# A two-layer diffusion trunk on one core: head products that take turns, attention in turns with dense projections, and one modulation round and the filter spectra at other places

## The chip, the cores and the metric

The kernel runs on one core of one Trainium2 chip. The metric is the time of one execution in device microseconds (us), a median over runs; lower is better. Below, PE is the matrix engine and PEld its weight loads, DVE the vector engine, ACT the scalar engine, POOL the general engine, and SP the engine whose queue issues nearly all DMAs.

## The reference, cut to what matters

Two trunk layers run over 256 latent tokens and 256 context tokens of width 1024. A layer is: modulation, one input projection whose columns go to attention, RWKV-7 and Hyena, one output projection, a norm, a channel mixer (dense SwiGLU in layer 0, top-2-of-8 experts in layer 1), a norm.

```python
for l in range(DEPTH):                      # DEPTH = 2
    need_ctx = l < DEPTH - 1
    mod_l = (cond_lat @ ada_w[l] + ada_b[l])[:, None, :]      # six vectors of 1024: sh1 sc1 g1 sh2 sc2 g2
    mod_c = (cond_ctx @ ada_w[l] + ada_b[l])[None, None, :]
    o_lat, o_ctx = token_mixer(modulate(x, sh1, sc1), modulate(xc, csh1, csc1), lp, rope, need_ctx)
    x = post_norm(alpha * x + g1 * o_lat, ln1_g[l], ln1_b[l])
    ...                                     # context: the same, in layer 0 alone
    f_lat = swiglu(...) if l % 2 == 0 else moe_swiglu(...)
    x = post_norm(alpha * x + g2 * f_lat, ln2_g[l], ln2_b[l])

def token_mixer(h_lat, h_ctx, lp, rope, need_ctx):
    u_lat = h_lat @ lp['w_in']; u_ctx = h_ctx @ lp['w_in']
    att_l, att_c = attention_group(...)     # latent queries read latent and context keys
    rw_l, rw_c = rwkv_group(...)            # latent scans start from the context scans' last states
    hy_l = hyena_group(u_lat[..., s_hy], lp)   # long convolution by spectra of filters (hyena_filter_spectrum)
    o_lat = jnp.concatenate([att_l, rw_l, hy_l], -1) @ lp['w_out']
    ...
```

## The kernel before, in words

Dense products are done in three passes of a split: `split` (L314 to L316) cuts an f32 operand into a high part (a cast on ACT, L315) and a rest (a subtraction on DVE, L316), and `mm3` (L318) sends three matmuls, L321, L322 and L323. `wload` fetches 512 KB of weights into a raw buffer (`raw`, L347, SP's queue) and splits it. The raw buffers are rings: six in the stage "l" (all of layer 0 and layer 1's context), five in the stage "n" (layer 1's latent mixer), thirty in the expert stage. `behind` keeps the order of loads in SP's queue as written. The order of the instructions on an engine is fixed when the kernel is built: a scheduler goes by the order in which the code emits them and by its own estimate of what is ready, so work emitted nearby is mixed. On the chip every engine runs its own list strictly in order.

What the tiles are called:

- `ada(l, rounds)` (L372) makes the modulation vectors: a round is 16 weight loads, each with four plain f32 matmuls of 32 weight columns (L392), a DVE addition, and four transposes `adaT`. `s.fill` hands such a round to `wload`, which takes one step of it with each weight load.
- `win_steps` (L466) is the input projection by tiles of 128 columns (`u`, 24 matmuls per tile). RW, ATT and HY are the tile lists of the three mixers; HY tiles are followed by a short convolution.
- `attend` (L755) yields after each half of a head pair: scores `aS`, the maximum on DVE, an exponential on ACT (`aP`), transposes `aPT`, the product with the values `ao`, the normaliser `azb`. A yield ends a turn where `go` (L1635) alternates several generators.
- `rw_dir` (L882) is one direction of RWKV: the triangular solve, then per token tile the chunk matrices `rM` (L1063) and `rN` (L1071, L1073), the serial scan `rS` (L1089), and `rZ` and `rY` (L1105 to L1124). It is run eight times, and each run does `rN` for two token tiles and four heads: 64 head turns in all. Two heads of a pair write to partitions 0 to 63 and 64 to 127 of one bank.
- `spectra(l, ...)` (L534) makes the filter spectra: `hf_d`, `hf`, two sines (`sn`, seven DVE instructions and one on ACT each), `hf_n`, `Kc`, `Ks`, `Kn`; it needs only weights, no token.
- `w_out` (L1295) is the output projection (`wo`) with its norm; `ffn` is the dense channel mixer (`ab`, then `fo`); `hT` (L445) normalises, transposes (L455) and splits an input.

Two calls of the RWKV code, `rwkv(0, ...)`, stand in layer 0 for the latent tokens and for the context, and two in layer 1. The calls around the change are all in `body` (L1676).

Of the kernel before, what the change touches and what calls it, by code (L numbers as in the profile page):

```python
# [251 lines left out]
CTX, LAT = 0, 1  # L252


def bc(ap, shape):
    return ap.to_broadcast(list(shape))
# [556 lines left out]
class Rwkv(Mix):  # L813
# [73 lines left out]
    def rw_dir(s, l, g, d, need_y):  # L887
# [3 lines left out]
        mm = nc.tensor.matmul  # L891
# [5 lines left out]
        for ct in range(2):  # L897
            for i in range(2):
                mm(ps[:, ct, i], g["th"][:, i, 256 * d + 128 * ct:256 * d + 128 * ct + 128], cum[:, d, :], start=True,
                   stop=True)  # L900
# [5 lines left out]
        for ct in range(2):  # L906
            mm(ps[:, ct], s.lora[l][32:64, 1, 256 * d + 128 * ct:256 * d + 128 * ct + 128], g["lora"][32:64, :],
               start=True, stop=True)
# [25 lines left out]
        for p in range(2):  # L934
            b = s.bank(f"w{d}", "rAB").rearrange("p (u m t) -> p u m t", u=4, m=4)
            r = slice(64 * p, 64 * p + 64)
            for tt in range(2):
                for ct in range(2):
                    for j in range(4):
                        o = slice(128 * tt + 32 * j, 128 * tt + 32 * j + 32)  # L940
                        for m, lh in ((0, kd), (2, be)):
                            mm(b[32 * j:32 * j + 32, 2 * tt + ct, m:m + W, :], lh[r, ct, o], kr[r, 0:W, ct, o],
                               start=True, stop=True)
# [13 lines left out]
        x = sub[:, 768:896].rearrange("p (u t) -> p u t", u=8)  # L957
# [19 lines left out]
        hv = lambda h: slice(64 * h, 64 * h + 64)  # L977
# [3 lines left out]
        kdt, bet = kbt[:, 0], kbt[:, 1]  # L981
        for tt in range(2):
            o = slice(128 * tt, 128 * tt + 128)
            b = s.bank(f"w{d}", "rtr")
# [5 lines left out]
        b = s.bank(f"w{d}", "rtr").rearrange("p (a c) -> p a c", a=2)  # L990
# [6 lines left out]
        b = s.bank(f"w{d}", "rAV").rearrange("p (i h v) -> p i h v", i=2, h=4)  # L997
# [10 lines left out]
        for i in range(1, 16):  # L1008
            t = i if d == 0 else 15 - i
# [14 lines left out]
        PQ = s.k([128, 2, 4, 2, 64], f"rPQ{d}")  # L1024
        done = [last]
        for step, w in enumerate((TT, BC, TT)):
            rhs = PQ if step == 1 else KA
            for tt in range(2):
                b = s.bank(f"w{d}", "rPQ")
                for h in range(4):  # L1030
                    mm(b[:, 128 * h:128 * h + 128], w[:, U(tt, h), :], rhs[:, tt, h].rearrange("p m v -> p (m v)"),
                       start=True, stop=True)
# [9 lines left out]
        bx = [s.k([128, 4, 256], f"rbx{d}") for _ in range(2)]  # L1042
        vx = g.get("vx")
        if vx is None:
            vx = g["vx"] = [s.k([128, 4, 256], "rvx") for _ in range(2)]
# [11 lines left out]
        for tt in range(2):  # L1057
            x = M[tt]
            s.order(nc.gpsimd.memset(x, 0.0), done[MX[tt]])
            b = s.bank(f"w{d}", "rM").rearrange("p (c j k) -> p c j k", c=2, j=4)  # L1060
            for h in range(4):
                r = slice(64 * (h % 2), 64 * (h % 2) + 64)
                mm(b[r, h // 2], PQ[:, tt, h, 0, :], bx[tt][:, :, hv(h)], start=True, stop=True)  # L1063
            for p in range(2):
                r = slice(64 * p, 64 * p + 64)
                nc.vector.tensor_add(x[r, :, r], b[r].rearrange("p c j k -> p (c j) k"),
                                     bc(s.c("ident")[r, r][:, None, :], [64, 8, 64]))
            b = s.bank(f"w{d}", "rN").rearrange("p (c j k) -> p c j k", c=2, j=4)
            for h in range(4):
                r = slice(64 * (h % 2), 64 * (h % 2) + 64)  # L1070
                mm(b[r, h // 2], kdt[:, tt, hv(h)], vx[tt][:, :, hv(h)], start=True, stop=True)  # L1071
                for j in range(4):
                    mm(b[r, h // 2, j, :], bx[tt][:, j, hv(h)], PQ[:, tt, h, 1, :], start=False, stop=True,  # L1073
                       skip_group_check=True)
            fed = nc.vector.tensor_mul(N[:, tt], b, bc(gc[:, :, 4 * tt:4 * tt + 4, None], [128, 2, 4, 64]))

        S = s.k([128, 8, 2, 64], f"rS{d}")
# [1 line left out]
        start = {}  # L1079
        prev = g["S0"][d] if g["S0"] else None  # L1080
        for i, ch in enumerate(order):
            tt, j = divmod(ch, 4)
# [3 lines left out]
            else:  # L1086
                b = s.bank(f"w{d}", "rS")[:, :128].rearrange("p (c v) -> p c v", c=2)
# [13 lines left out]
        b = s.bank(f"w{d}", "rZ").rearrange("p (c t) -> p c t", c=2)  # L1101
        for tt in range(2):
            for h in range(4):
                r = slice(64 * (h % 2), 64 * (h % 2) + 64)
                mm(b[r, h // 2, 128 * tt:128 * tt + 128], PQ[:, tt, h, 0, :], BD[3][:, U(tt, h), :], start=True,  # L1105
                   stop=True)
# [3 lines left out]
        for p in range(2):  # L1110
            b = s.bank(f"w{d}", "rY")[:, :256].rearrange("p (i c v) -> p i c v", i=2, c=2)
            r = slice(64 * p, 64 * p + 64)
            for tt in range(2):
                for ct in range(2):
                    h = 2 * ct + p
                    i = mm(b[:, tt, ct, :], BD[1][:, U(tt, h), :], vt[:, tt, hv(h)], start=True, stop=True)
                    if tt == 0 and ct == 0:
# [3 lines left out]
                       skip_group_check=True)  # L1121
                    for j in chs:
                        c0 = 128 * tt + 32 * j
                        mm(b[32 * j:32 * j + 32, tt, ct, :], Z[r, ct, c0:c0 + 32], start[4 * tt + j][r, ct, :],  # L1124
                           start=False, stop=True, skip_group_check=True)
# [77 lines left out]
class Ffn(Rwkv):  # L1203
# [63 lines left out]
        return ms, rs, last  # L1267

    def tok_mm(s, src, ts, banks, nk, khs=None):

        for n, kh in enumerate(khs or range(nk // 2)):
            hi, lo = s.wload(src(kh))
            if n == s.LAG:
                s.flush()
            for i in range(len(banks))[::1 - 2 * (kh % 2)]:
                for k in (2 * kh, 2 * kh + 1):
                    ns = slice(512 * (k % 2), 512 * (k % 2) + 512)
                    s.mm3(banks[i], ts(i, k), (hi[:, ns], lo[:, ns]), k == 0, k == nk - 1)

    def tok_last(s, chunks, ts, nk):  # L1280

# [10 lines left out]
        if f:  # L1292
            f()

    def w_out(s, l, st, oT, x, halves=False):  # L1295


        ts = lambda i, k: tuple(t[:, 128 * i:128 * i + 128] for t in oT[k])
        banks = []

        def product(h, khs=None):
            s.tok_mm(lambda kh: s.A["wout"][l, h, kh], ts, banks[h], 8, khs)

        def o(h):
            if halves:
                banks.append([s.bank("g", "wo") for _ in range(2)])
                product(h)
            elif h == 0:
                banks.extend([[s.bank("g", "wo") for _ in range(2)], [s.bank(f"w{i}", "wo") for i in range(2)]])
                for h2 in range(2):  # L1310
                    product(h2, [0, 1, 2])
                s.tok_last([(s.A["wout"][l, h2, 3], 3, banks[h2]) for h2 in range(2)], ts, 8)
            yield
            return banks[h]

        return s.whole(s.post_norm(l, st, 0, x, [o], () if halves else (0, 1)))


    def block(s, b, hp):
# [248 lines left out]
class Top(Ffn):  # L1568
# [58 lines left out]
    def whole(s, gen):  # L1627

        while True:
            try:  # L1630
                next(gen)
            except StopIteration as e:
                return e.value

    def go(s, *gens):  # L1635

        gens = [g if isinstance(g, tuple) else (1, g) for g in gens]
        while gens:
            for q in list(gens):
                for _ in range(q[0]):  # L1640
                    if next(q[1], s) is s:
                        gens.remove(q)
                        break
# [14 lines left out]
    def body(s):  # L1658
        RW, HY, ATT = [0, 1, 2, 3, 4, 7, 8], [13, 14, 15, 16, 17, 18], [5, 6, 9, 10, 11, 12]
        s.setup()  # L1660
        s.w = "a"
        ada = s.ada(0, [0])
        s.some(ada, 3)
        s.ldcst(1)
        s.some(ada, 5)
        with s.behind():
            x = s.ldx(CTX)
        for _ in ada:
            pass
        s.w = "l"  # L1670
        sp = s.spectra(0, "w0", "t", "w1", *s.sp)
        next(sp)
        oT = []
        s.ldlora(0)

        def start(st, x):  # L1676
            g = {"st": st, "h": s.hT(0, st, 0, x)}
            if st == 0:
                next(sp)
            oT.append(s.pairs("oTa", "oTa", "oTr", "oTh"))  # L1680
            s.win(0, RW, g)
            for n in (3, 4) if st == 0 else ():
                s.ldcst(n)
            return g


        g = start(CTX, x)
        s.rw_prep(0, g)
        s.win(0, HY, g)
        S0 = s.rwkv(0, g, None, oT[CTX])  # L1690
        s.fill = s.ada(0, [1, 2])
        s.go(s.hyena(0, g, oT[CTX]))
        s.win(0, ATT, g)
        with s.behind():
            x = s.ldx(LAT)

        gl = start(LAT, x)
        s.go(s.attend(0, g, oT[CTX]))
        s.rw_prep(0, gl)
        s.win(0, HY, gl)  # L1700
        s.rwkv(0, gl, S0, oT[LAT])
        s.win(0, ATT, gl)
        s.go(s.attend(0, gl, oT[LAT]))
        x = [s.w_out(0, CTX, oT[CTX], None, True)]
        s.go(s.hyena(0, gl, oT[LAT]))
        s.drain()
        f = s.ffn(0, CTX, x[CTX])
        s.some(f, 1)
        x.append(s.w_out(0, 1, oT[1], None))
        s.fill = s.ada(1, [0, 1, 2])  # L1710
        xc = s.whole(f)
        s.drain()
        f = s.ffn(0, LAT, x[LAT])
        s.some(f, 10)

        s.ldlora(1)
        gc = {"st": CTX, "h": s.hT(1, CTX, 0, xc)}
        s.win(1, [0, 1, 2, 3, 4, 5, 6], gc)
        s.rw_prep(1, gc)
        S0 = s.rwkv(1, gc, None, None)  # L1720
        sp = s.spec_load(1)
        x = s.whole(f)

        s.w = "n"
        gl = {"st": LAT, "h": s.hT(1, LAT, 0, x)}
        for _ in s.spectra(1, "w0", "t", "w1", *sp()):
            pass
        oT = s.pairs("oTa", "oTa", "oTr", "oTh")
        s.win(1, RW, gl)
        s.rw_prep(1, gl)  # L1730
        s.rwkv(1, gl, S0, oT)
        s.win(1, ATT + HY[:2], gl)
        s.go(s.attend(1, gl, oT))
        s.win(1, HY[2:], gl)
        s.go(s.hyena(1, gl, oT))
        x = s.w_out(1, LAT, oT, x)
        s.w = "m"
        s.moe(1, x)
# [18 lines left out]
```

## Time and profile before

| | us |
|---|---|
| median of 3 runs | 2132.26 |
| lowest and highest | 2120.98, 2132.55 |
| the profiled execution: its time, its span | 2140.86, 2139.1 |

Its mean granted clock of PE is 0.959 of full speed. In the rows, a window is a stretch in us from the span's start, and it gives the busy time of each engine in it (number of instructions), the granted clock, the share of the DMA engines and GB/s. PE's matmuls overlap, so the mean duration of one is longer than the step from one to the next.

### The profile page before, as it was taken

Reading aid. Unit: us, or ns where it says so; the run is one execution under the profiler, and the core shown is the slowest. Engines: PE = TensorE matmul, PEld = TensorE weight load, DVE = VectorE, ACT = ScalarE, POOL = GpSimd, SP = SyncE. Lnnn points to the kernel's source line nnn. Section 1 sums busy time; section 2 is a strip of 40 time slices with the busy share of each in tenths; the row PEclk is TensorE's granted clock in tenths of the full one; section 3 lists DMA queues with packets and bytes.
Section 4 is the critical chain, followed back from the end, with each engine's and each line's share of the span. In section 5 each row is a group of like instructions: output and inputs, shape, how many; then the busy total and the mean of one; then the engine's idle time right before and its main releaser. Section 6 shows DMA issues by size and latency. Waiting matters only on the chain. (4 is left out here: it accounts for less than half of the span.)

```text
span 2139.1 us, 35418 instructions
## 1 busy us (share of the span) xinstructions
PE 2044.7 (96%) x13514; PEld 1668.0 (78%) x13514; DVE 1659.1 (78%) x3050; ACT 1102.6 (52%) x1613; POOL 106.2 (5%) x87
## 2 busy tenths in 40 slices
PE   8999999999999999989798997999999999999996
PEld 3878777768877999978577676888888888888885
DVE  7786678459744595685888568799899989998997
ACT  3532445132333434443354232777787877778773
POOL 0022001100000000010002200000000000000000
PEclk9999899799999999999898997999999999999998
DMA  8422333146698535422311038699999999999992
GB/s 323 164 82 90 139 124 82 59 155 223 231 341 298 197 131 198 165 83 95 128 60 53 30 110 315 216 322 361 355 346 367 354 341 351 366 356 342 364 353 105
DMA packets 147850, 469.12 MB, mean 219 GB/s; under 512 B 31636, under 2 KB 33972, under 8 KB 147672
## 3 DMA queue, kind: packets, MB, share of 16 engines
q1 hardware_dynamic: 123512, 446.27, 57.6%
q0 software_dynamic: 4816, 17.36, 2.2%
q10 hardware_dynamic: 19344, 3.15, 0.8%
q8 instruction: 108, 1.77, 0.3%
q14 instruction: 70, 0.57, 0.1%
HBM read 464.56 MB, written 2.16 MB: 218 GB/s over the span
## 5 line engine op out<-in xcount | busy, mean ns | idle before, releaser
L316 DVE TENSOR_TENSOR wlo<-wraw,whi 128x1024 fp32r<-128x1024 f32 x748 | 885.3, 1219 | 87.4 <-ACT whi L315 58.7
L315 ACT CAST whi<-wraw 128x1024 fp32r<-128x1024 f32 x748 | 751.2, 1049 | 132.8 <-DMA wraw<-in_fw_dram 39.0
L321 PE MATMUL ab<-whi,m_x 128*128 128x512 f32 x704 | 281.6, 400 | 0.0
L323 PE MATMUL ab<-whi,m_x 128*128 128x512 f32 x704 | 275.6, 391 | 0.0
L322 PE MATMUL ab<-wlo,m_x 128*128 128x512 f32 x704 | 275.0, 391 | 0.0
L321 PE MATMUL ab<-hp,whi 128*128 128x256 f32 x704 | 205.2, 293 | 3.1 <-ACT hp L315 2.2
L323 PE MATMUL ab<-hp,wlo 128*128 128x256 f32 x704 | 201.7, 288 | 4.0 <-DVE wlo L316 4.0
L322 PE MATMUL ab<-hp,whi 128*128 128x256 f32 x704 | 201.5, 287 | 1.3 <-DVE hp L316 1.1
L321 PE MATMUL u<-hp,whi 128*128 128x256 f32 x512 | 153.7, 303 | 2.7 <-ACT hp L315 2.5
L323 PEld LDWEIGHTS ab<-whi,m_x 128*128 128x128 f32 x704 | 132.2, 188 | 28.3
L322 PEld LDWEIGHTS ab<-wlo,m_x 128*128 128x128 f32 x704 | 132.5, 188 | 25.5 <-DVE wlo L316 0.2
L321 PEld LDWEIGHTS ab<-whi,m_x 128*128 128x128 f32 x704 | 132.2, 188 | 25.1
L323 PE MATMUL u<-hp,wlo 128*128 128x256 f32 x512 | 150.8, 297 | 1.0 <-DVE wlo L316 1.0
L322 PE MATMUL u<-hp,whi 128*128 128x256 f32 x512 | 151.4, 298 | 0.0
L321 PEld LDWEIGHTS ab<-hp,whi 128*128 128x128 f32 x704 | 136.2, 194 | 18.9 <-issue 11.0
L323 PEld LDWEIGHTS ab<-hp,wlo 128*128 128x128 f32 x704 | 136.4, 194 | 5.8 <-DVE wlo L316 5.3
L322 PEld LDWEIGHTS ab<-hp,whi 128*128 128x128 f32 x704 | 136.7, 194 | 2.0 <-DVE hp L316 1.8
L321 PE MATMUL mo<-whi,ffg 128*128 128x512 f32 x352 | 137.8, 392 | 0.0
L323 PE MATMUL mo<-whi,ffg 128*128 128x512 f32 x352 | 137.1, 390 | 0.0
L322 PE MATMUL mo<-wlo,ffg 128*128 128x512 f32 x352 | 137.0, 389 | 0.0
L321 PEld LDWEIGHTS u<-hp,whi 128*128 128x128 f32 x512 | 101.2, 199 | 18.7 <-issue 10.3
L969 POOL TENSOR_TENSOR rBD<-rAT,cst 128x1024 f32<-128x1024 f32 x28 | 66.3, 2373 | 889.7 <-issue 523.5
(396 smaller groups left out, 3550.5 us busy)
## 6 DMA issues: line engine op xcount, KB each, us to landing
wraw<-in_mw_dram SPq DMA_DIRECT2D x495, 512.0 KB, 5.6
wraw<-in_fw_dram SPq DMA_DIRECT2D x132, 512.0 KB, 5.5
wraw<-in_adaw_dram SPq DMA_DIRECT2D x96, 512.0 KB, 4.7
wraw<-in_win_dram SPq DMA_DIRECT2D x64, 512.0 KB, 4.8
wraw<-in_mw_dram POOLq DMA_DIRECT2D x33, 512.0 KB, 6.8
wraw<-in_wout_dram SPq DMA_DIRECT2D x24, 512.0 KB, 4.3
lngb<-in_rows_dram SPq DMA_DIRECT2D x12, 512.0 KB, 7.1
x<-in_xs_dram SPq DMA_DIRECT2D x8, 512.0 KB, 5.4
```

Of the source, the lines that this page charges most:

```text
L315: i = (s.nc.scalar.copy if eng == "a" else s.nc.vector.tensor_copy)(hi, src)
L316: return i, s.nc.vector.tensor_sub(lo, src, hi.bitcast(F32))
L321: mm(out, a[0], b[0], start=start, stop=False, **kw)
L322: mm(out, a[0], b[1], start=False, stop=False, **kw)
L323: mm(out, a[1], b[0], start=False, stop=stop, **kw)
L969: i = nc.gpsimd.tensor_mul(x.rearrange("p u (j t) -> p u j t", j=4), bc(ATu[:, :, m, None, :], [128, 8, 4, 32]), bc(mask.rearrange("p (j t ...
```

## The change

Five things change. First, in `rw_dir` the four heads' `rN` products are written so that the two heads of a pair alternate matmul by matmul. Second, `w_out` can be run in steps (`w_out_steps`, over `tok_steps`; a turn is one weight load), and `into` stores its result. Third, attention takes turns with a dense projection in three places: the context's attention of layer 0 with the latent HY tiles (the attention stood before `rw_prep`), the latent attention of layer 0 with the context's output projection (which followed it), and the latent attention of layer 1 with all six HY tiles (two of them stood before it, four behind). Fourth, the third round of layer 1's `ada` is no longer part of the filling of the context's channel mixer, but runs at once where the latent channel mixer has ended. Fifth, layer 1's spectra, with all their loads, are emitted before the rest of the latent channel mixer, no longer behind the latent `hT` of layer 1.

```diff
             b = s.bank(f"w{d}", "rN").rearrange("p (c j k) -> p c j k", c=2, j=4)
-            for h in range(4):
-                r = slice(64 * (h % 2), 64 * (h % 2) + 64)
-                mm(b[r, h // 2], kdt[:, tt, hv(h)], vx[tt][:, :, hv(h)], start=True, stop=True)
+            for c in range(2):
+                for p in range(2):
+                    h = 2 * c + p
+                    mm(b[64 * p:64 * p + 64, c], kdt[:, tt, hv(h)], vx[tt][:, :, hv(h)], start=True, stop=True)
                 for j in range(4):
-                    mm(b[r, h // 2, j, :], bx[tt][:, j, hv(h)], PQ[:, tt, h, 1, :], start=False, stop=True,
-                       skip_group_check=True)
+                    for p in range(2):
+                        h = 2 * c + p
+                        mm(b[64 * p:64 * p + 64, c, j, :], bx[tt][:, j, hv(h)], PQ[:, tt, h, 1, :], start=False,
+                           stop=True, skip_group_check=True)
...
     def tok_mm(s, src, ts, banks, nk, khs=None):
+        for _ in s.tok_steps(src, ts, banks, nk, khs):
+            pass
+
+    def tok_steps(s, src, ts, banks, nk, khs=None):
         for n, kh in enumerate(khs or range(nk // 2)):
             hi, lo = s.wload(src(kh))
...
                     s.mm3(banks[i], ts(i, k), (hi[:, ns], lo[:, ns]), k == 0, k == nk - 1)
+            yield
...
+    def into(s, out, gen):
+        out.append((yield from gen))
...
         gl = start(LAT, x)
-        s.go(s.attend(0, g, oT[CTX]))
         s.rw_prep(0, gl)
-        s.win(0, HY, gl)
+        s.go(s.attend(0, g, oT[CTX]), s.win_steps(0, HY, gl))
         s.rwkv(0, gl, S0, oT[LAT])
         s.win(0, ATT, gl)
-        s.go(s.attend(0, gl, oT[LAT]))
-        x = [s.w_out(0, CTX, oT[CTX], None, True)]
+        x = []
+        s.go(s.attend(0, gl, oT[LAT]), s.into(x, s.w_out_steps(0, CTX, oT[CTX], None, True)))
...
-        s.fill = s.ada(1, [0, 1, 2])
+        s.fill = s.ada(1, [0, 1])
...
         S0 = s.rwkv(1, gc, None, None)
-        sp = s.spec_load(1)
+        for _ in s.spectra(1, "w0", "t", "w1", *s.spec_load(1)()):
+            pass
         x = s.whole(f)
+        for _ in s.ada(1, [2]):
+            pass
         s.w = "n"
         gl = {"st": LAT, "h": s.hT(1, LAT, 0, x)}
-        for _ in s.spectra(1, "w0", "t", "w1", *sp()):
-            pass
...
-        s.win(1, ATT + HY[:2], gl)
-        s.go(s.attend(1, gl, oT))
-        s.win(1, HY[2:], gl)
+        s.win(1, ATT, gl)
+        s.go(s.attend(1, gl, oT), s.win_steps(1, HY, gl))
```

Three places of the built order. On PE, in the `rN` of the first direction in layer 0's latent RWKV, before (lines of the kernel before, `rM`, `aS`, `ada` and `aPT` being other work that the scheduler put between):

```order
L392 MATMUL ada_2934<-wraw_4606,keep_66 32x256
L1063 MATMUL rM_3462<-rbx0_3409,rPQ0_3371 64x256 x3
L774 MATMUL aS_4324<-akv_1866,aq_4052 128x512
L774 MATMUL aS_4325<-akv_1866,aq_4052 128x512
L1063 MATMUL rM_3462<-rbx0_3409,rPQ0_3371 64x256
L392 MATMUL ada_2934<-wraw_4606,keep_66 32x256 x3
L1071 MATMUL rN_3469<-rvx_3411,rkbt0_3265 64x256
L1073 MATMUL rN_3469<-rPQ0_3371,rbx0_3409 64x64 x4
```

The same `rN` tile in the changed kernel, whose lines are L1073 for the wide product and L1077 for the narrow ones:

```order
L392 MATMUL ada_2812<-wraw_4289,keep_66 32x256 x4
L321 MATMUL wo_4281<-whi_4285,oTa_392 128x512
L1073 MATMUL rN_3469<-rvx_3411,rkbt0_3265 64x256 x2
L1077 MATMUL rN_3469<-rPQ0_3371,rbx0_3409 64x64 x6
L774 MATMUL aS_4307<-akv_1866,aq_4052 128x512
L774 MATMUL aS_4308<-akv_1866,aq_4052 128x512
L1077 MATMUL rN_3469<-rPQ0_3371,rbx0_3409 64x64 x2
```

Before, one head's wide and four narrow products stood together, and the next head's behind them; now two wide ones stand together, and eight narrow ones in which the heads alternate.

On PE, from the last matmul of layer 0's latent channel mixer (`fo`) to the first products of layer 1's latent projection (`u`), before:

```order
L323 MATMUL fo<-whi,ffg 128x512
L542 MATMUL hf_10450<-cst_68,sn 64x256
L548 MATMUL hf_d<-hydec,cst_68 128x512
L563 MATMUL hf_d<-hyd,cst_68 128x512
L557 MATMUL hf_10471<-sn 64x256
L455 MATMUL hT<-keep,xhat 128x128 x2
L575 MATMUL hf_10490<-hy_10446,sn 128x512
L455 MATMUL hT<-keep,xhat 128x128 x6
L575 MATMUL hf_10494<-hy_10446,sn 128x512
L575 MATMUL hf_10505<-hy_10446,sn 128x512
L455 MATMUL hT<-keep,xhat 128x128 x4
L321 MATMUL u<-hp,whi 128x256
```

And in the changed kernel:

```order
L323 MATMUL fo<-whi,ffg 128x512
L392 MATMUL ada<-wraw,keep 32x256 x44
L455 MATMUL hT<-keep,xhat 128x128
L392 MATMUL ada<-wraw,keep 32x256 x4
L455 MATMUL hT<-keep,xhat 128x128
L392 MATMUL ada<-wraw,keep 32x256 x4
L455 MATMUL hT<-keep,xhat 128x128 x6
L392 MATMUL ada<-wraw,keep 32x256 x4
L455 MATMUL hT<-keep,xhat 128x128 x4
L392 MATMUL ada<-wraw,keep 32x256 x4
L455 MATMUL hT<-keep,xhat 128x128 x4
L392 MATMUL ada<-wraw,keep 32x256 x4
```

The spectra's products are gone from here, and the 64 matmuls of the modulation round stand here, 44 of them before the first transpose `hT` and the rest among the transposes; the four transposes `adaT` and then the projection's `u` follow behind the last row. In SP's queue the sixteen loads of the round now stand in front of the loads of layer 1's latent projection (`in_win`):

```order
L347 DMA wraw<-in_fw_dram 128x1024 x26
L1214 DMA lngb<-in_rows_dram 128x1024
L347 DMA wraw<-in_adaw_dram 128x1024 x2
L1214 DMA lngb<-in_rows_dram 128x1024
L347 DMA wraw<-in_adaw_dram 128x1024
L385 DMA ada<-in_adab_dram 128x512
L347 DMA wraw<-in_adaw_dram 128x1024 x13
L347 DMA wraw<-in_win_dram 128x1024 x12
```

Before, the channel mixer's last 26 loads were followed by the last load of the spectra and then at once by those of the projection.

On PE, in the serial scan `rS` of the second direction of layer 0's latent RWKV, where the latent attention runs too, before:

```order
L1089 MATMUL rS<-rS_3747,rMx_3685 128x64 x2
L788 MATMUL aPT<-keep,aP 128x128 x2
L1089 MATMUL rS<-rS_3747,rMx_3684 128x64 x2
L788 MATMUL aPT<-keep,aP 128x128 x4
L795 MATMUL ao<-aPT,akv 64x256
L1089 MATMUL rS<-rS_3747,rMx_3684 128x64 x2
L795 MATMUL ao<-aPT,akv 64x256 x2
L774 MATMUL aS<-akv,aq 128x512 x2
L795 MATMUL ao<-aPT,akv 64x256 x5
L1089 MATMUL rS<-rS_3747,rMx_3684 128x64 x2
```

And in the changed kernel:

```order
L1093 MATMUL rS<-rS_3747,rMx_3685 128x64 x2
L322 MATMUL wo<-wlo,oTr 128x512
L323 MATMUL wo<-whi,oTr 128x512
L321 MATMUL wo<-whi,oTr 128x512
L322 MATMUL wo<-wlo,oTr 128x512
L323 MATMUL wo<-whi,oTr 128x512
L321 MATMUL wo<-whi,oTr 128x512
L1093 MATMUL rS<-rS_3747,rMx_3684 128x64 x2
L322 MATMUL wo<-wlo,oTr 128x512
L323 MATMUL wo<-whi,oTr 128x512
```

Between the steps of the scan there now stand dense products of the context's output projection, where attention's small products stood alone.

## Rows read from the trace of the kernel before

**Rows 1.** Windows: us, then busy us of PE, PEld, DVE, ACT, POOL, PEclk, DMA, GB/s.

```profile
150.00:1045.00 895.00, 871.21 (x6880) 722.23 (x6880) 597.62 (x1313) 333.87 (x556) 49.83 (x28) 0.96 0.46 163
500.00:700.00 200.00, 198.59 (x1497) 159.07 (x1496) 124.50 (x230) 64.32 (x78) 0.00 (x0) 1.00 0.75 269
1000.00:1042.80 42.80, 42.80 (x261) 37.27 (x257) 30.95 (x51) 15.16 (x18) 0.00 (x0) 1.00 0.52 190
```

**Rows 2.** PE's groups by line and form: count, busy us, mean ns of one.

```profile
L1071 PE MATMUL rN<-rvx,rkbt 128*64 128x256 f32 x128 | 41.2, 403 | 0.0
L1073 PE MATMUL rN<-rPQ,rbx 128*64 128x64 f32 x512 | 40.9, 222 | 0.0
L1063 PE MATMUL rM<-rbx,rPQ 128*64 128x256 f32 x128 | 19.7, 392 | 0.7 <-ACT rPQ L1039 0.7
L1105 PE MATMUL rZ<-rBD,rPQ 128*64 128x128 f32 x96 | 7.8, 303 | 0.0
L942 PE MATMUL rAB<-rkr,rkdb 64*32 64x64 f32 x768 | 15.9, 219 | 0.7 <-issue 0.4 <-DVE rkdb L928 0.3
L392 PE MATMUL ada<-wraw,keep 128*32 128x256 f32 x768 | 73.5, 402 | 0.0
```

**Rows 3.** Window of the whole span, instructions of the tile rN alone: PE, PEld, DVE.

```profile
0.00:2139.10 2139.10, 53.51 (x640) 42.70 (x640) 40.97 (x140) 0.96 0.61 219
```

**Rows 4.** Windows around layer 1's latent norm, columns as in rows 1.

```profile
1042.80:1071.10 28.30, 16.47 (x49) 8.28 (x48) 25.88 (x92) 7.30 (x15) 0.00 (x0) 0.64 0.11 38
1042.80:1048.00 5.20, 2.55 (x7) 0.85 (x6) 5.17 (x20) 1.74 (x3) 0.00 (x0) 1.00 0.01 2
```

**Rows 5.** Timeline of PE and SP there: start us, us, what, idle before it.

```profile
1042.48 0.39 PE L323 MATMUL fo<-whi,ffg 128*128 128x512 f32 x1
1057.80 0.69 PE L455 MATMUL hT<-keep,xhat 128*128 128x128 f32 x2 [4.75 <-DVE xhat L441]
1071.07 0.51 PE L321 MATMUL u<-hp,whi 128*128 128x256 f32 x2
1019.59 79.70 SPq L347 DMA_DIRECT2D wraw<-in_win_dram  x12
```

**Rows 6.** The spectra's groups in 1042.8 to 1071.1 and in 1071 to 1092 (PE).

```profile
L575 PE MATMUL hf<-hy,sn 64*128 64x512 f32 x8 | 7.0, 994 | 0.5 <-ACT sn L513 0.5
...
L548 PE MATMUL hf_d<-hydec,cst 1*128 1x512 f32 x2 | 1.1, 640 | 0.0
...
L595 PE MATMUL Kc<-hy_eo,cst 128*128 128x512 f32 x8 | 3.9, 592 | 0.0
L600 PE MATMUL Ks<-hy_eo,cst 128*128 128x512 f32 x8 | 3.9, 592 | 0.0
L582 PE MATMUL hf_n<-hy_ab,cst 128*128 128x512 f32 x4 | 2.1, 618 | 0.5 <-POOL hy_ab L581 0.5
L606 PE MATMUL Kn<-hy_eo,cst 128*32 128x512 f32 x4 | 1.9, 598 | 0.0
```

**Rows 7.** The largest of the two sines' groups on DVE in 1042.8 to 1061.

```profile
L511 DVE SCALAR_TENSOR_TENSOR sn<-sn 64x256 f32<-64x256 f32 x6 | 2.4, 399 | 0.0
...
L503 DVE TENSOR_SCALAR sn<-hf,keep 64x256 f32<-64x256 f32 x2 | 1.1, 527 | 0.0
```

**Rows 8.** Loads of ada weights (KB each, us to landing), and a window of dense loading.

```profile
wraw<-in_adaw_dram SPq DMA_DIRECT2D x96, 512.0 KB, 4.7
590.00:600.00 10.00, 10.00 (x90) 8.88 (x87) 3.20 (x4) 3.07 (x4) 0.00 (x0) 1.00 1.03 415
```

**Rows 9.** Windows of the attention stretches, columns as in rows 1.

```profile
404.00:434.00 30.00, 29.48 (x173) 20.34 (x171) 9.56 (x29) 3.67 (x10) 2.33 (x1) 0.54 0.24 88
450.00:470.00 20.00, 18.00 (x109) 12.16 (x109) 15.23 (x42) 8.38 (x17) 0.00 (x0) 1.00 0.27 99
1180.00:1265.00 85.00, 79.29 (x660) 54.75 (x659) 47.75 (x123) 23.08 (x53) 11.23 (x6) 0.92 0.11 38
228.00:300.00 72.00, 71.34 (x512) 51.29 (x512) 49.48 (x138) 35.34 (x83) 0.00 (x0) 0.90 0.28 103
```

More of the change, by code (lines that the diff above doesn't have):

```diff
@@ L1293, in flush, with w_out, w_out_steps @@
             f()
-    def w_out(s, l, st, oT, x, halves=False):
+    def w_out(s, l, st, oT, x):
+        return s.whole(s.w_out_steps(l, st, oT, x))
+    def w_out_steps(s, l, st, oT, x, halves=False):
         ts = lambda i, k: tuple(t[:, 128 * i:128 * i + 128] for t in oT[k])
         banks = []
-        def product(h, khs=None):
-            s.tok_mm(lambda kh: s.A["wout"][l, h, kh], ts, banks[h], 8, khs)
+        src = lambda h: lambda kh: s.A["wout"][l, h, kh]
         def o(h):
@@ L1306, in o @@
                 banks.append([s.bank("g", "wo") for _ in range(2)])
-                product(h)
+                yield from s.tok_steps(src(h), ts, banks[h], 8)
             elif h == 0:
@@ L1310, in o @@
                 for h2 in range(2):
-                    product(h2, [0, 1, 2])
+                    s.tok_mm(src(h2), ts, banks[h2], 8, [0, 1, 2])
                 s.tok_last([(s.A["wout"][l, h2, 3], 3, banks[h2]) for h2 in range(2)], ts, 8)
@@ L1314, in o @@
             return banks[h]
-        return s.whole(s.post_norm(l, st, 0, x, [o], () if halves else (0, 1)))
+        return s.post_norm(l, st, 0, x, [o], () if halves else (0, 1))
     def block(s, b, hp):
```

## The prediction

> **What bounds the kernel now.** I read the windows first, because the mean over the span hides the stages. From 150 to 1045 us PE is busy 871.21 of 895 us while DVE is busy two thirds of that time; in the context's channel mixer (500 to 700) PE is busy 198.59 of 200, and in the latent one's end 42.80 of 42.80, both at full clock [rows 1]. So PE sets the pace of nearly everything, and a change can win in three ways only: PE needs less time for the same work, PE waits less, or PE's clock is lowered for a shorter time. The second look is therefore at windows with a wait or a low clock. One is layer 1's latent norm: from the last product of the channel mixer (1042.8) to a steady flow of the next projection (1071.1) 28.3 us pass in which PE is busy 16.47 us at a mean clock of 0.64 [rows 4, 5]. Others are the attention stretches: 404 to 434 runs at 0.54 though PE is busy 29.48 of 30 us, 450 to 470 leaves PE idle for 2 us, and 1180 to 1265 has 5.7 us idle at a clock of 0.92 [rows 9]. The third look is at PE's groups by form, for work that is slower than its like [rows 2]. The expert stage (from about 1345 us) is untouched by the change and I cost it at nothing.
>
> **Head turns in `rN`.** Nothing is added or removed: 128 records of the wide product and 512 of the narrow one stay [rows 2]. The wide one has the very form of `rM` (128 by 64 weights, 256 columns), where the two heads already alternate: `rM` takes 19.7 us for 128 records, `rN`'s wide product 41.2 [rows 2]. The group times overlap in part, since `rN` as a whole is busy 53.51 us [rows 3]. With turns I take 19.7 us for the wide part. For the narrow part (64 columns) the nearest row is `rZ`, which alternates heads with 128 columns at 7.8 / 96 = 81 ns per record; half the columns give 41 ns, so 512 x 41 = 21 us. Together 40.7, against 53.5: 12.8 us less. The ends: nothing (a head's last narrow products already run beside the next head's first wide one), and 19.7 + 512 x 20 ns (the step of `rAB`, 15.9 / 768, the fastest narrow product here) = 30, so 23.5 us less. What lies on the path: in two of the three stages with `rN` PE is nearly full, but around the scans it waits for DVE anyway, so I count three quarters: **-9.6 us** (0 to -23.5).
>
> The Trainium skill bears on this in "TensorEngine Tiling (Array Packing)", sections Theoretical Speedup and Key Properties: 64-column tiles work independently, with up to twice the speed. By that rule 53.5 would become 26.7 and the term about -20; `rM` beside `rN` agrees with it for wide products, and no row here shows two alternating products of 64 by 64. The sum goes by my rows.
>
> **The modulation round and the spectra, taken together.** Four amounts change.
> (a) A round of `ada` costs PE 73.5 / 6 = 12.2 us [rows 2]. It leaves the context's channel mixer, where PE has no room: -12.2.
> (b) The spectra's second half (`Kc`, `Ks`, `hf_n`, `Kn`: 3.9 + 3.9 + 2.1 + 1.9 = 11.8 us) leaves layer 1's projection at full clock: -11.8 [rows 6].
> (c) The latent norm. Today DVE is the chain there: it is busy 5.17 of the first 5.2 us and 25.88 of the 28.3 [rows 4], and among it are the two sines, 14 DVE instructions with 2.4 + 1.1 us in two of their five groups [rows 7]; I take 4 us for both. Without them the first `hT` moves from 15.0 us behind the last `fo` (1057.80 - 1042.80) to about 11.5, the last to below 20. What is late next is the round's own loading. Six raw buffers are filled ahead; each frees after 12.2 / 16 = 0.77 us of PE work, and ten more loads follow, the first about 4.7 us after its issue and then one each 512 KB / 415 GB/s = 1.3 us [rows 8]: 0.8 + 4.7 + 9 x 1.3 = 17 us after the last `fo`. The projection's loads now stand behind them in SP's queue; before, they were issued from 1019.59 on, long in advance [rows 5]. The first comes one step later (18.5), and the split takes ACT and DVE some 2 us more: `u` flows from about 20.5 us on, not 28.3. In the old 28.3 some 2 us of `u` were already done, so: -5.9. With everything ahead of time this could be -12; if the loads come in two full batches with their latency between them, nothing.
> (d) The spectra now stand in the latent channel mixer, where PE is full: 11.8 us for the second half, and for the first 7.0 us for `hf` and four small groups of about 1 us like `hf_d` [rows 6], 11 us at a mean clock of 0.64 or 7 at full clock. With 3 us for waits of a PE in strict order on the spectra's chain over DVE, ACT and POOL (which now runs beside a DVE that is already busy 30.95 of 42.80 us, rows 1): +11.8 + 7 + 3 = +21.8 (18.8 to 27).
> Sum: -12.2 - 11.8 - 5.9 + 21.8 = **-8.1 us** (+3 to -17).
>
> **Attention in turns with dense products.** No instruction is added. In layer 0's latent attention the loss to be won is (1 - 0.54) x 30 = 13.8 us of clock, 0.5 us idle, and 2 us idle from 450 to 470: 16.3 us [rows 9]. In the new order `wo` stands between the steps of the scan and of attention, but two blocks of `rY` still stand almost alone, so I keep 7 us of the loss: **-9** (0 to -15). In layer 1, 1180 to 1265 loses 5.7 us idle and 0.08 x 85 = 6.8 us of clock [rows 9]; the HY tiles fill half: **-6** (0 to -12). The context's attention of layer 0 loses 0.7 us idle and 0.10 x 72 = 7 us of clock, which I put down mostly to RWKV work before it: **-1** (+2 to -5). What hides the tiles' ACT and DVE work: DVE is busy 47.75 of 85 us there [rows 9]. What is queued behind a wait: in strict order a `wo` or `u` that waits for its bank (three banks serve `u`, `wo` and `ao`) holds attention behind it.
>
> In "TensorE: Matmul & The Clock Gate", HAM clock gate, the Trainium skill has the clock fall from 2.4 to 1.2 GHz after an idle stretch. The row of 404 to 434 differs: 0.54 with PE busy 98% of the time. By the page, covering a PE that is not idle would give no clock back; the measurement decides for the sum, and the page's way is the second rival.
>
> **The sum.** -9.6 - 8.1 - 9 - 6 - 1 = -33.7 us against the profiled execution's 2140.86: 2107. That execution lies 8.6 us above the median of 2132.26, so against the median: 2132.3 - 33.7 = **2098.6 us**.
>
> **Rivals.** Under 1% (21 us) I call no change, about what a measurement of this kernel tells from none.
> 1. More than I count: the turns reach 20 us (narrow products at the step of `rAB`), the norm 12, the attention stretches 20: 2132 - 52 = 2080. For it: `rM`, which halves; against: waits of the scan on DVE, which stay.
> 2. The clock stays low: the small products of RWKV, not the lack of filling, lower it, and `rY` still stands in a block. Attention then gives back only idle time, 2 + 0.5 in layer 0 and 3 in layer 1, instead of 16: 2132 - 9.6 - 8.1 - 5.5 = 2109, and with half the turns 2114. For it: the low clock at a busy PE; against: the dense `wo` inside the stretch.
> 3. The turns do nothing, because consecutive narrow products are held by their weight loads (PEld is busy 42.70 us in `rN`, rows 3): 2132 - 24 = 2108. With rival 2 as well: 2118.
> 4. Slower: the bank turns. Attention now shares three banks with a dense product that holds two of them in layer 0. There are 24 half-pair turns (four pairs, two halves, three places). If PE, in strict order, stands still in each for a part of the chain from scores to transposes, the gain of 34 is eaten at 1.4 us per turn; at 2.4 us per turn it is 58 - 34 = 24 us slower: 2156. For it: PE can't pass a waiting instruction; against: the scheduler placed about one to six dense products in each turn, and PE waits on attention's own chain for under 3 us in all in 450 to 470 today.
>
> **How the numbers follow.** Chances: the forecast with its own spread (2085 to 2111) 0.50; rival 1 0.15; rivals 2 and 3 where they leave under 1% 0.25; rival 4 in mild form (within 1% of before) 0.02, in full 0.08. Faster by over 1% means below 2111: 0.65. Within 1%: 0.27. Slower: 0.08. The range holds 8 in 10: it reaches down to 2074 for most of rival 1 and up to 2126 for most of rivals 2 and 3, and leaves out the slower end.
>
> **What would show it.** Right: `rN` busy about 41 us instead of 53.5; no spectra between the last `fo` and the next `u`, that stretch near 20 us with the clock near full; in the scan of layer 0's second latent direction a clock near 0.8 or more; PE idle in the latent attention of layer 1 below 3 us. Wrong: `rN` unchanged; PE waiting for ada weights among the `hT`; PE waiting for a sine or for POOL inside the latent channel mixer for over 5 us; PE waiting before `wo`, `u` or `ao` for a bank; a clock of 0.5 for as long as before.

## The result and the profile after

The changed kernel takes 2112.53 us (median of 4 runs, 2108.68 to 2115.96) against 2132.41 for before: ratio 0.9899, interval 0.9867 to 0.9931. That is 20 us less, 14 more than the 2098.6 forecast and inside the range. Its profiled execution took 2110.26 us (span 2108.5, mean clock 0.968), 30.6 less than the one of before.

To see where, I cut the span at marks that both kernels have: the context's first `rPQ` in layer 0, the latent direction's last `rAB`, the first `ab` of the context's channel mixer, its last `fo`, the latent channel mixer's last `fo`, the first `rAB` of layer 1's latent direction, the router's first product. The windows between them, after (columns as in rows 1):

```profile
149.00:320.20 171.20, 164.20 (x1579) 130.61 (x1579) 120.91 (x317) 67.20 (x149) 18.32 (x10) 0.92 0.32 111
320.20:514.40 194.20, 190.50 (x1387) 142.41 (x1386) 147.03 (x404) 69.35 (x136) 20.54 (x11) 0.96 0.40 136
514.40:730.10 215.70, 213.47 (x1582) 184.78 (x1579) 132.28 (x203) 79.62 (x93) 0.00 (x0) 0.99 0.65 236
730.10:1032.90 302.80, 289.85 (x2293) 253.38 (x2295) 220.77 (x432) 126.39 (x192) 16.95 (x10) 0.99 0.43 150
1032.90:1092.90 60.00, 49.43 (x419) 39.53 (x417) 49.15 (x130) 25.90 (x44) 0.00 (x0) 0.89 0.39 136
1092.90:1281.00 188.10, 176.05 (x1548) 141.46 (x1547) 134.97 (x369) 69.61 (x141) 23.86 (x14) 0.95 0.36 122
```

And before, in the same cut:

```profile
143.50:319.50 176.00, 173.43 (x1600) 136.14 (x1599) 122.25 (x319) 68.20 (x150) 18.35 (x10) 0.92 0.32 110
319.50:525.10 205.60, 197.34 (x1360) 149.00 (x1360) 139.96 (x400) 67.57 (x135) 20.37 (x11) 0.93 0.39 125
525.10:753.30 228.20, 226.78 (x1717) 187.74 (x1715) 133.59 (x209) 79.74 (x94) 0.00 (x0) 1.00 0.72 259
753.30:1042.90 289.60, 277.56 (x2250) 253.24 (x2248) 206.19 (x402) 120.50 (x184) 13.37 (x8) 0.98 0.40 144
1042.90:1115.30 72.40, 59.98 (x328) 42.10 (x329) 61.31 (x156) 29.53 (x50) 2.74 (x2) 0.86 0.15 52
1115.30:1310.90 195.60, 181.98 (x1546) 145.55 (x1546) 136.50 (x369) 69.34 (x141) 23.80 (x14) 0.93 0.28 94
```

Six stages, in order: -4.8, -11.4, -12.5, +13.2, -12.4, -7.5. The start (5.5 longer) and the expert stage (0.7 shorter) make up the rest of -30.6. These are differences of one profile each; further profiles, below, leave little of the first two and half of the last. `rN`'s PE time, the counterpart of [rows 3], fell as worked out (53.51 to 39.54, forecast 40.7); the window of the tile `rN` alone, after:

```profile
0.00:2108.50 2108.50, 39.54 (x640) 29.60 (x640) 41.87 (x140) 0.97 0.62 222
```

The gap of layer 1's latent norm on PE, after, answers to [rows 5] (start us, us, what, idle before it):

```profile
1032.47 0.39 PE L323 MATMUL fo<-whi,ffg 128*128 128x512 f32 x1
1032.79 4.96 PE L392 MATMUL ada<-wraw,keep 128*32 128x256 f32 x88
1045.29 0.47 PE L455 MATMUL hT<-keep,xhat 128*128 128x128 f32 x1 [7.55 <-DVE xhat L441]
...
1054.27 0.66 PE L404 MATMUL adaT<-keep,ada 128*128 128x128 f32 x4 [1.53 <-DVE ada L397]
...
1056.77 0.54 PE L321 MATMUL u<-hp,whi 128*128 128x256 f32 x1 [1.21 <-ACT whi L315]
```

SP had issued all sixteen loads of the round by 1025.45, before its first product (start us, us from the first issue to the end of the last):

```profile
985.70 4.45 SPq L347 DMA_DIRECT2D wraw<-in_adaw_dram  x2
993.93 0.33 SPq L347 DMA_DIRECT2D wraw<-in_adaw_dram  x1
1004.42 21.03 SPq L347 DMA_DIRECT2D wraw<-in_adaw_dram  x13
```

PE goes through eleven of them (88 records, 8 to a load) without a wait, up to the first `hT` of its list. There it stands 7.55 us for DVE's norm, not for a load, and `u` flows 24 us after the last `fo`.

### The profile page after: what moved, and what is told of

It reads as the page before. It is cut to its first block, busy times and chain, and to the rows that moved or that the text cites. A ratio compares the mean times of both kernels' runs of the same rounds, so it can differ in the third digit from the quotient of the medians.

```text
span 2108.5 us, 35471 instructions
## 1 busy us (share of the span) xinstructions
PE 2015.0 (96%) x13514; PEld 1644.5 (78%) x13514; DVE 1663.9 (79%) x3050; ACT 1106.1 (52%) x1615; POOL 107.2 (5%) x87
```

## The experiments

All times stand against before in the same comparison. Two sums help: a run's time multiplied by its mean granted clock (its work, as if all of it ran at full clock), and the rest, its clock loss. They are sums of mine, and rough ones, since waits for DVE or DMA don't scale with PE's clock. Clocks and sums of several runs are medians.

**Head turns alone.** Edit: the first hunk of the change and nothing else.

```diff
-            for h in range(4):
...
+            for c in range(2):
+                for p in range(2):
+                    h = 2 * c + p
...
```

> The kernel before with the head turns in rN alone. The forecast's term says -9.6 us (rN busy 53.5 -> about 40 us, three quarters of it on the path). First rival: the 14 us of rN come back as waits of the scans on DVE, so rN is busy about 40 us but the time moves by less than 3 us. Second rival, that weight loads hold the narrow products: rN stays above 48 us and the time is unchanged. In the stages: the context's layer 0 from rPQ to the latent direction's last rAB was 176.0 us before and 171.2 with the whole change; if the turns alone did that, it is about 171 here.

Measured: 2144.18 (10 runs) against 2133.03 (17 runs), ratio 1.0043, interval 1.0012 to 1.0073: slower, by 9 us (3 to 16). `rN` is busy 38.73 us. The mean clock of the runs is 0.957 against 0.966: the work falls by 7.6 us (2051.3 from 2058.9), the clock loss grows by 20 (92.2 from 72.7). PE's waits from 150 to 240 us show what becomes of the shorter block (us in total, times, longest):

```profile
PE rS L1093 <- DVE rS L1095: 3.4, 1, 3.4
PE rS L1093 <- DVE rS L1089: 1.9, 1, 1.9
```

In before the scan waits there once, for 0.3 us:

```profile
PE rS L1089 <- DVE rS L1091: 0.3, 1, 0.3
```

Neither of my theories had the clock in it.

**Attention turns alone**, at all three places; edit: the change in `body` for them, and the step functions.

```diff
-        s.go(s.attend(0, g, oT[CTX]))
...
-        s.win(0, HY, gl)
+        s.go(s.attend(0, g, oT[CTX]), s.win_steps(0, HY, gl))
...
```

> The kernel before with attention in turns with dense projections alone (all three places). The forecast's terms say -9 -6 -1 = -16 us: the stretch from layer 0's last rAB to the first ab of the context's channel mixer falls from 205.6 to about 194 us, that from layer 1's rAB to the router from 195.6 to about 189. Rival 2 (the clock stays low, only idle time is covered): -5.5 us in all, 205.6 -> about 203 and 195.6 -> about 192.5. Rival 4 (bank turns cost): no gain or slower, PE waiting ahead of wo, u or ao.

Measured: 2120.54 (8 runs), ratio 0.9937, interval 0.9907 to 0.9967: -13 us (-7 to -20). The work falls by 6 us, the clock loss by 8. Rival 4 is out, and the 5.5 us of rival 2 lie just outside the interval. Most of the profile's gain stands in the first stage, where I had -1, then in the second; the sixth, layer 1, did not move (before: 176.00, 205.60 and 195.60):

```profile
141.00:302.00 161.00, 158.73 (x1586) 124.23 (x1586) 119.96 (x319) 67.13 (x149) 18.07 (x10) 1.00 0.35 121
302.00:499.50 197.50, 190.77 (x1379) 144.03 (x1377) 146.25 (x402) 68.83 (x136) 21.62 (x12) 0.97 0.40 131
1090.20:1285.70 195.50, 184.63 (x1548) 148.33 (x1547) 137.14 (x369) 69.51 (x141) 23.76 (x14) 0.92 0.35 120
```

In the sixth PE's idle time fell from 13.6 to 10.9 us, the clock from 0.93 to 0.92.

**Round and spectra, together and apart.** Edits: the two hunks of the change that stand ahead of its last; then the halves. The round's half is printed here, the spectra's is the rest: all of `spectra` ahead of `x = s.whole(f)`.

```diff
-        s.fill = s.ada(1, [0, 1, 2])
+        s.fill = s.ada(1, [0, 1])
...
+        for _ in s.ada(1, [2]):
+            pass
```

> The kernel before with the modulation round moved to the latent norm's gap and all spectra among the latent channel mixer's products, nothing else. The forecast's four terms sum to -8.1 us: context channel mixer 228.2 -> 216, last context fo to last latent fo 289.6 -> about 311, last latent fo to layer 1's rAB 72.4 -> about 55. The trace of the whole change says instead 215.7, 302.8 and 60.0, together -11.7 us; if its stages are additive this kernel shows that.

> The kernel before with the modulation round alone moved to the latent norm's gap; the spectra stay behind the first hT. Forecast's terms: -12.2 in the context's channel mixer; the gap stays as long as before, since DVE's norm and sines pace it, so about -12 in all and 2121. If the round's 5 us of matmuls at the gap's start and its DVE work push the first hT and the sines back, the stretch from the last latent fo to layer 1's rAB grows from 72 to about 80 and the gain is about -5.

> The kernel before with the spectra alone moved among the latent channel mixer's products; all three rounds stay in the context's channel mixer. Forecast's terms: +21.8 in the latent channel mixer (+16 by the trace of the whole change), -11.8 in layer 1's projection and -4 to -8 for the gap: from +6 to -4, so 2129 to 2139. If the rise of the clock that the runs of both moves show (0.974 against 0.966) comes from the spectra, this is 2120 or less at a mean clock above 0.970; if from the round, the clock stays at 0.966.

Measured: together 2112.08 (4 runs), ratio 0.9890 (0.9841 to 0.9939); the round alone 2127.34 (10 runs), 0.9973 (0.9942 to 1.0004); the spectra alone 2135.97 (10 runs), 1.0008 (0.9984 to 1.0033). The first three and the fifth stage with both:

```profile
148.70:314.10 165.40, 162.87 (x1600) 127.35 (x1599) 121.87 (x319) 68.05 (x150) 18.36 (x10) 0.99 0.34 118
314.10:506.60 192.50, 185.34 (x1361) 140.76 (x1361) 140.03 (x400) 67.72 (x135) 20.36 (x11) 0.99 0.40 134
506.60:721.20 214.60, 213.19 (x1585) 183.94 (x1583) 132.67 (x205) 79.67 (x93) 0.00 (x0) 1.00 0.67 237
721.20:1029.00 307.80, 295.85 (x2292) 259.59 (x2294) 220.77 (x432) 126.35 (x192) 16.79 (x10) 0.98 0.45 149
1029.00:1088.90 59.90, 49.34 (x419) 39.55 (x419) 49.15 (x130) 25.89 (x44) 0.00 (x0) 0.91 0.38 127
```

Channel mixers and gap sum to -13.6 + 18.2 - 12.5 = -7.9. The gap stage took 78.1 us with the round alone and 53.2 with the spectra alone (72.4 before): the round lengthens it by 5.7, the spectra's leaving shortens it by 19.2, and both together give what the two add up to, within 1 us. The first two stages are 23.7 us shorter than in before, though PE's order in them is the same: only the clock differs (0.99 against 0.92 and 0.93). Over the four runs of both together the work falls by 4 us and the clock loss by 18 (clock 0.974, before 0.966); neither half alone moves the clock (0.967 and 0.966, before 0.965). What each half does to the time in all is not shown, since both intervals reach 1.

**Before once more.** No edit.

> The kernel before once more, nothing edited, for a second profile. Two things that the forecast read from one profile are asked: the clock loss of layer 0 (0.73 to 0.55 in 190 to 240, 0.50 in 410 to 430, about 27 us from 180 to 440) and the start (first u at 43.8 us). If the clock dips belong to the order of the work, as the forecast took them, they stand at the same places again. If they are drawn anew in each execution, layer 0 looks different: the kernel with the round and the spectra moved alone has the same order of layer 0 and showed it 24 us shorter, with no dip there.

Measured: 2130.08 (8 runs), ratio 1.0003. The profiled span is 2124.5, 14.6 us below the first, and the first two stages of this second profile of the same program are:

```profile
145.40:318.60 173.20, 170.58 (x1600) 133.81 (x1599) 122.16 (x319) 68.09 (x150) 18.35 (x10) 0.94 0.32 112
318.60:511.10 192.50, 185.29 (x1361) 140.74 (x1361) 139.97 (x400) 67.67 (x135) 20.38 (x11) 0.99 0.42 135
```

Together 15.9 us shorter, while the four stages that follow agree within 0.4 us each. Length times clock agrees: 162 and 191 in the first profile, 163 and 191 in the second. The dip at 404 to 434 is not there:

```profile
404.00:434.00 30.00, 29.59 (x318) 20.95 (x318) 12.97 (x39) 6.84 (x17) 2.34 (x1) 1.00 0.50 177
```

It was drawn in that execution: of five profiles with the same order of PE in layer 0 (before twice, the round, the spectra, both), two have it, before's first and that of the spectra alone (0.59 there). Against this second profile the changed kernel's first two stages are not 4.8 and 11.4 us shorter, but 2.0 shorter and 1.7 longer. Nor is the draw mere noise. In the three profiles without head turns whose first stage begins at 145.4 to 145.6 us (this one, the first without turns, the filled gap) the clock is 0.83 from 200 to 210, 0.72 to 0.74 from 220 to 230 and 0.58 to 0.60 from 230 to 240; in the three that begin it at 148.7 to 149.2 (the round, both, the second without turns) it is 1.00 in all three windows. In these six, dips go with the moment at which the stage begins; why, no run shows.

**The change without its head turns**, twice; edit: `rN` as before, all else as changed.

> The changed kernel without the head turns: rN as before, the round, the spectra and attention as changed. By the forecast's term the head turns are worth 9.6 us, so this should take about 2112 + 9.6 = 2122. By the runs of single parts (head turns alone 2144.2 against 2133.0, with the mean clock of the runs 0.957 against 0.966) they cost about 11 us by lowering the clock, so this should take about 2101, with a mean clock near 0.975.

> The changed kernel without head turns once more, beside the changed kernel on the same chip, for the verdict between the two. By the first comparison 2104; by the forecast's term for head turns it should be 9.6 us slower than the changed kernel.

Measured: 2104.06 and 2106.20 (6 runs each), ratios 0.9866 (0.9830 to 0.9901) and 0.9870 (0.9830 to 0.9910). The changed kernel itself, measured two more times:

> The changed kernel once more, nothing edited. About -20 us against before, as in its own comparison. Its profiled start (first u at 50.5 us against 43.8 in before, in code that is the same) is the question: if that is chance of the loading, a second profile shows another number, anywhere between 43 and 51 us; if the changed program causes it, again about 50.5.

> The changed kernel once more, nothing edited, as the partner of the run without head turns: about 2112, mean clock 0.965, against 2104 and 0.975 for the kernel without head turns. If the two are alike here, the head turns cost nothing that can be measured.

Measured: 2111.49 and 2112.12, ratios 0.9879 (0.9829 to 0.9929) and 0.9882 (0.9839 to 0.9924). The intervals overlap, so that the turns cost some 3 us here by the ratios, 6 to 7 by the medians, is likely and not shown; that they don't win 9.6 us is (means of 2111.0 in 14 runs with them, 2107.1 in 12 without). The clock is plainer: 0.973 and more in 10 of 12 runs without turns, at most 0.968 in all 14 with them. Over these 26 runs the work falls by 16 us with the turns and the clock loss grows by 23, much as on the kernel before. The sixth stage takes 192.1 and 191.6 us in the two later profiles of the changed kernel, so that of its -7.5 in the first some 4 were drawn. (The first `u` came at 50.2 and 51.0 us again, but at 43.8 and 48.5 in before's two profiles, and at 50.1 to 50.5 in the round, the spectra and both, whose code up to there is before's: the changed program does not cause it, and what does stays open.)

**Turns with padding.** Edit, ahead of the turned loop:

```diff
+            for c, p in ((0, 0), (0, 1), (1, 0)):
+                h = 2 * c + p
+                mm(b[64 * p:64 * p + 64, c], kdt[:, tt, hv(h)], vx[tt][:, :, hv(h)], start=True, stop=True)
```

> The changed kernel, head turns kept, with three wide products of each rN block issued once more ahead of the block (their sums are overwritten, so nothing of the result changes): some 48 products of about 0.31 us, 15 us, so that rN is busy about 54 us again, as before the change. It asks why the head turns lower the clock. Theory idle: the shorter rN leaves PE waiting for DVE (7 to 10 us idle from rPQ to the latent direction's rAB, 2.5 without turns), and the clock falls after it; then the padding brings the idle time back to about 3 us and the mean clock to about 0.974, and the time to about 2104 to 2108 although 15 us of work are added. Theory density: two heads on the array at once are what lowers the clock; then the clock stays at 0.965 or below and the time is 2115 or more.

Measured: 2116.56 (11 runs), ratio 0.9919 (0.9888 to 0.9950), mean clock 0.970, `rN` busy 54.26 us. Between the two theories: with 15 us of work added, the time rose by some 4. Windows of the kernel with head turns alone, first, and of the padded one:

```profile
180.00:190.00 10.00, 7.39 (x38) 6.60 (x38) 5.51 (x18) 1.05 (x1) 1.75 (x1) 0.66 0.16 52
...
230.00:240.00 10.00, 10.00 (x73) 7.77 (x72) 2.70 (x9) 1.71 (x5) 0.00 (x0) 0.68 0.44 140
240.00:250.00 10.00, 10.00 (x33) 7.41 (x34) 5.86 (x14) 4.19 (x9) 0.00 (x0) 0.50 0.15 55
```

```profile
180.00:190.00 10.00, 8.82 (x91) 7.67 (x91) 6.71 (x20) 2.14 (x5) 3.46 (x2) 1.00 0.23 63
...
230.00:240.00 10.00, 10.00 (x48) 6.66 (x51) 2.20 (x7) 2.72 (x6) 0.00 (x0) 0.50 0.31 104
240.00:250.00 10.00, 10.00 (x40) 7.14 (x39) 4.98 (x12) 1.66 (x3) 0.00 (x0) 0.50 0.29 107
```

The padding more than halves the idle time at 180 to 190 (2.6 to 1.2 us), and the dip is gone. All four profiles with turns and no padding have this dip (0.66 to 0.68), the other ten have 1.00 there. In a finer cut, again the head turns alone and then the padded kernel, the clock falls to half right behind the idle stretch, and with the padding it does not:

```profile
179.00:183.00 4.00, 0.65 (x10) 0.51 (x6) 3.86 (x10) 0.00 (x0) 2.75 (x2) 0.94 0.10 20
183.00:189.00 6.00, 6.00 (x35) 5.76 (x35) 2.09 (x9) 1.05 (x1) 0.00 (x0) 0.50 0.20 74
```

```profile
179.00:183.00 4.00, 2.82 (x32) 2.02 (x30) 3.44 (x7) 0.00 (x0) 2.09 (x1) 1.00 0.02 4
183.00:189.00 6.00, 6.00 (x64) 5.40 (x59) 3.79 (x13) 1.79 (x3) 2.37 (x1) 1.00 0.23 74
```

The dip at 230 to 250, with PE always busy, stays. It needs no head turns: four of the nine profiles without them have one there too (0.55 to 0.60 from 230 to 240), before's first for one:

```profile
230.00:240.00 10.00, 10.00 (x37) 7.41 (x37) 5.41 (x15) 4.70 (x11) 0.00 (x0) 0.55 0.01 2
```

So the waits that the faster `rN` opens explain a part of the lower clock (0.970 lies between 0.966 and 0.976), and the rest stays open: whether it lies in two heads on the array at once, this run does not tell, since its padding is turned too.

**The gap filled.** Edit, on the kernel without head turns: `spectra` stops ahead of the last products; they are issued in the gap, each eviction ordered behind the norm.

```diff
-        for _ in s.spectra(1, "w0", "t", "w1", *s.spec_load(1)()):
-            pass
+        sp = s.spectra(1, "w0", "t", "w1", *s.spec_load(1)(), split=True)
+        s.some(sp, 2)
         x = s.whole(f)
         for _ in s.ada(1, [2]):
             pass
+        next(sp)
...
-        s.win(1, RW, gl)
+        s.win(1, RW[:3], gl)
+        for _ in sp:
+            pass
+        s.win(1, RW[3:], gl)
...
```

> The kernel without head turns (2104) with the spectra's last products (Kc, Ks, Kn: 9.7 us of PE) taken out of the latent channel mixer and put into the latent norm's gap, where PE stands idle 7.6 us for the norm on DVE; their evictions are ordered behind the norm. If the gap is DVE's and has room, the last part of the latent channel mixer shrinks by about 9 us and the gap grows by 1 to 4: -5 to -8, about 2097. If the products' evictions (two of 0.65 us between the norm and the hT) and the queue of ada products hold the hT back, the gap grows by as much as is won: 2104.

Measured: 2098.72 (6 runs, 2094.32 to 2099.80), ratio 0.9831, interval 0.9794 to 0.9867; beside it on the same chip 2106.20 without the filling and 2112.12 for the changed kernel. Its fourth and fifth stages, and PE where the wait stood:

```profile
725.40:1022.90 297.50, 285.40 (x2273) 254.81 (x2272) 215.43 (x422) 125.12 (x190) 16.79 (x10) 0.98 0.45 154
1022.90:1081.30 58.40, 56.12 (x440) 39.82 (x439) 53.80 (x140) 26.62 (x45) 0.00 (x0) 1.00 0.35 134
```

```profile
1022.87 2.80 PE L392 MATMUL ada<-wraw,keep 128*32 128x256 f32 x48
1025.60 1.98 PE L595 MATMUL Kc<-hy_eo,cst 128*128 128x512 f32 x4
...
1035.35 0.33 PE L456 MATMUL hT<-keep,xhat 128*128 128x128 f32 x1 [0.70 <-DVE xhat L441]
```

The kernel without the filling has 305.6 and 59.9 us in these two stages, a clock of 0.91 in the second, and a wait of 7.5 us for `xhat`, which is 0.70 here: the products have left a mixer in which PE was full, and the gap has not grown. The ratios' intervals overlap, but on this chip each of the six runs with the filling is shorter than each of the six without. Of all kernels run it is the fastest.

## Why the prediction was right, and where it was not

The total came within 14 us, with terms that failed in both directions: head turns alone some 19 us worse than forecast, round and spectra 13 better, attention 3 worse. That they largely cancel is luck.

- **Head turns, -9.6.** The PE time was right to 1.2 us, and the work fell by 8 and 16 us in the two pairs of kernels. The step that failed is "what lies on the path": a block that ends sooner was counted at three quarters, with nothing as the worst end. Alone the turns lose 3 to 16 us; in the changed kernel a loss is likely and a gain of 9.6 ruled out. In both pairs the clock took back more than the work won, 20 and 23 us, of which the waits for DVE explain a part. The bound "nothing" left out that a faster block can open waits and change the clock. Rival 3's size was right for a reason that was wrong: the turns do work. By the Trainium skill ("TensorEngine Tiling (Array Packing)", Theoretical Speedup) up to a factor of 2 was open; `rN` gained 1.35.
- **Round and spectra, -8.1.** Right in the sum of the stages (-7.9), less so in each: (a) -12.2, measured -12.5 with the whole change and -13.6 with this part alone; (d) +21.8, measured 18.2 alone and 13.2 beside the head turns; (b) and (c) together -17.7, measured -12.4. Within (c) the step "what is late next is the round's own loading" failed: all sixteen loads, not six, were issued before the round began, and PE waited 7.55 us for `xhat`, so that the first `hT` came 12.8 us behind the last `fo` and not 11.5. That the whole part timed -21 instead of -8 is mostly the clock (18 us by the sums), in its one profile that of layer 0, whose order it does not touch. All four of its runs had 0.969 to 0.976. Against chance speaks that the twelve runs without head turns, which hold this part and attention, have 0.976 where attention alone has 0.970; the cause stays open.
- **Attention, -9, -6, -1.** Measured in all -13 alone, and some -4 to -8 as the part added last (2104 and 2106, ratios 0.9866 and 0.9870, against 2112 and 0.9890 for round and spectra alone; the intervals overlap). The sign and the order of size hold, the places don't. The 13.8 us of clock at 404 to 434 [rows 9] were read from one execution, and the second one of the same program doesn't have them. In layer 1 PE's idle time shrank, the clock did not rise, and the stage stayed as long: the -6 was not there (the changed kernel's later profiles have 3.5 and 4.0 us less).
- **The reference.** I set the forecast against the median since that profiled execution lay 8.6 us above it. The same observation should have told me that its dips were not all the kernel's own.
- **The clock.** The dip at 180 to 190 follows an idle stretch and went when the stretch was shortened; that at 230 to 250 stands with PE busy 10.00 of 10 us. The page "TensorE: Matmul & The Clock Gate" of the Trainium skill (HAM clock gate) lets the clock fall after idle stretches: the first dip agrees, the second it does not explain.

## What to carry to other kernels

Before a term is read from a low clock, take a second profile of the same kernel: stages whose length times clock agrees while their length does not are drawn, and a change can't be credited with them. A faster block on an engine that bounds the kernel is not worth its busy time if what follows waits for another engine (here 14 us less of `rN` made the kernel 9 us slower): look first at who feeds the next instruction, and time that part alone. And where an engine stands idle for a chain that can't be shortened, move work there that has its own operands and its own bank, from a place where that engine is full (here 7 us).

## What the runs showed of the hardware

- Executions of one program differ by up to 30 us (before: 2114.29 to 2144.71 in 29 runs), and the mean granted clock goes with it (0.971 in the shortest, 0.959 in the longest).
- A reordering of the same instructions can change the mean clock: 0.957 with head turns (10 runs) against 0.966 without (17), 0.966 (14) against 0.976 (12) on the changed kernel.
- The clock was at 0.50, the lower of its two levels, right behind a stretch from 179 to 183 us in which PE was busy 0.65 of 4 us, and also in a window in which PE was busy 10.00 of 10 us.
- In two profiles of one program, stages of 176.0 and 173.2 us, and of 205.6 and 192.5, agree within 1 us once multiplied by their clock.
